# Splitting the first load of a half-rotary kernel into a one-row DMA and a fifteen-row DMA

## The chip, the cores and the metric

The kernel runs on one core of a Trainium2 chip. Its time is the device time of one execution in microseconds (us). Before the change three runs took 161.86, 161.61 and 161.78 us, a median of 161.78 us.

## What is computed

The input x has the shape (16, 512, 16, 64) in float32: batch, sequence, heads, dimension. cos and sin have the shape (512, 32), of which only the first 16 columns count. Of the 64 numbers of a head the first 32 are rotated in two halves of 16, and the last 32 are copied.

```python
x1, x2 = x[..., :32], x[..., 32:]
first  = x1[..., :16] * cos[..., :16] - x1[..., 16:] * sin[..., :16]
second = x1[..., :16] * sin[..., :16] + x1[..., 16:] * cos[..., :16]
return np.concatenate([first, second, x2], axis=-1)
```

So 33.55 MB are read and 33.55 MB are written, with about three operations for each rotated number.

## The kernel before

**Tiling.** x is seen as 16 x 512 = 8192 rows of 1024 floats (4 KB each). A tile t (0 to 3) is 128 partitions times K = 16 consecutive rows, so a partition of a tile is one contiguous run of 64 KB in memory, and a tile is 8.39 MB. Three tiles fit in the SBUF buffer `ring` (slot t mod 3); the fourth tile goes into slot 0 when tile 0 has been written out. `rows(t, lo, hi)` at L51 names rows lo to hi of a tile in all partitions, and `load` (L54) and `store` (L57) make one DMA of them.

**The DMA queues.** All loads and the stores of tiles 0, 1 and 3 are issued by SyncE (SP), in the order of the program; the page counts their packets under queue q1. The small loads of cos and sin (L63, L64) and the store of tile 2 are issued by GpSimd (POOL), under queue q0. Both queues are served by the same 16 DMA engines. An SP instruction that waits for a semaphore holds everything behind it on SP.

**The order of SP's work.** It issues load(0), load(1) and the second half of load(2) at once (L65 to L67). Then it waits for the rotated tile 0 and issues store(0) (L107), and behind it the first half of load(2) (L108). load(3) (L109) waits until store(0) has landed, since both use slot 0. store(1) (L112) is held by a dependency written out by hand (L118) until a part of tile 2 is rotated, so that it stands behind load(3) at the DMA engines. store(3) (L126) is the last.

**The tables.** The 64 KB of cos and of sin arrive in 32 partitions of `stage`. VectorE (DVE) waits for both (L73), shuffles and copies them (L73, L80, L83) into `table`, in which every partition has the 16 rows of cos and sin that belong to its 16 rows of x. This takes from 15.83 to 21.19 us of the profiled execution.

**The rotation.** `rotate(t, lo, hi)` (L90) is four DVE instructions on rows lo to hi: two products (L96, L97), a difference (L98) and a sum (L101). A half tile (8 rows) takes 4.43 + 4.42 + 2.29 + 2.28 us. The first product, L96, waits for the load of its rows; all later instructions follow on DVE in the program's order.

Of the kernel before, what the change touches and what calls it, by code (L numbers as in the profile page):

```python
# [1 line left out]

# [4 lines left out]


@with_exitstack
def kernel(  # L10
    ctx: ExitStack,
    tc: tile.TileContext,
    x: bass.AP,
    cos: bass.AP,
    sin: bass.AP,
    out: bass.AP,
):
    nc = tc.nc
    fp32 = mybir.dt.float32
    P = 128  # L20
    B, S, H, D = x.shape
    Q = D // 4
    HF = D // 2

    K = 16
    T = B * S // (P * K)
    PB = S // K
    REP = P // PB  # L30
    R = H * D
    NS = 3
    KC = K // 2
    KM = 5

    xf = x.rearrange("b s h d -> (b s h d)").rearrange("(t p f) -> t p f", t=T, p=P)
    of = out.rearrange("b s h d -> (b s h d)").rearrange("(t p f) -> t p f", t=T, p=P)
    cosf = cos.rearrange("(p k) j -> p (k j)", k=K)
    sinf = sin.rearrange("(p k) j -> p (k j)", k=K)

    const_pool = ctx.enter_context(tc.tile_pool(name="const", bufs=1))
    b_pool = ctx.enter_context(tc.tile_pool(name="bp", bufs=1, space=bass.MemoryType.PSUM))


    ring = const_pool.tile([P, NS, K, H, D], fp32)
    stage = const_pool.tile([P, 2, K, HF], fp32)
    spun = const_pool.tile([P, 2 * K, Q], fp32)
    packed = const_pool.tile([PB, 2 * K, Q], fp32)
    table = const_pool.tile([P, 2, K, 2, Q], fp32)

    def rows(t, lo, hi):  # L51
        return ring[:, t % NS, lo:hi].rearrange("p k h d -> p (k h d)")

    def load(t, lo=0, hi=K):  # L54
        return nc.sync.dma_start(out=rows(t, lo, hi), in_=xf[t, :, lo * R : hi * R])

    def store(t, lo=0, hi=K, queue=nc.sync):  # L57
        return queue.dma_start(out=of[t, :, lo * R : hi * R], in_=rows(t, lo, hi))  # L58


    nc.vector.memset(stage[:, :, :, 0:Q], 0.0)  # L61
    spread = stage.rearrange("(j b) t k i -> j b t (k i)", b=REP)
    nc.gpsimd.dma_start(out=spread[:, 0, 0], in_=cosf)  # L63
    nc.gpsimd.dma_start(out=spread[:, 0, 1], in_=sinf)  # L64
    load(0)  # L65
    load(1)
    load(2, KC, K)  # L67

    PQ = PB // REP
    nc.vector.stream_shuffle(  # L73
        out=spun[:],
        in_=stage.rearrange("p t k j -> p (t k) j")[:, :, 0:Q],
        mask=[j % PQ * REP for j in range(PB)],
    )
    for q in reversed(range(REP)):
        n = PQ * (q + 1)
        nc.vector.tensor_copy(out=packed[0:n], in_=spun[q * PB : q * PB + n])  # L80

    for r in range(REP):
        nc.vector.tensor_copy(  # L83
            out=table[r * PB : (r + 1) * PB].rearrange("p t k c j -> p (t k) c j"),
            in_=packed.unsqueeze(2).to_broadcast((PB, 2 * K, 2, Q)),
        )
    C = table[:, 0].rearrange("p k c j -> p k (c j)")
    Sn = table[:, 1].rearrange("p k c j -> p k (c j)")

    def rotate(t, lo, hi):  # L90
        x1 = ring[:, t % NS, lo:hi, :, 0:HF]
        c = C[:, lo:hi].unsqueeze(2).to_broadcast((P, hi - lo, H, HF))
        s = Sn[:, lo:hi].unsqueeze(2).to_broadcast((P, hi - lo, H, HF))
        b_full = b_pool.tile([P, KC, H, HF], fp32, name="b_t")
        b_t = b_full[:, 0 : hi - lo]
        nc.vector.tensor_mul(out=b_t, in0=x1, in1=s)  # L96
        nc.vector.tensor_mul(out=x1, in0=x1, in1=c)  # L97
        nc.vector.tensor_sub(  # L98
            out=x1[:, :, :, 0:Q], in0=x1[:, :, :, 0:Q], in1=b_t[:, :, :, Q:HF]
        )  # L100
        return nc.vector.tensor_add(  # L101
            out=x1[:, :, :, Q:HF], in0=x1[:, :, :, Q:HF], in1=b_t[:, :, :, 0:Q]
        )

    rotate(0, 0, KC)
    rotate(0, KC, K)
    store(0)  # L107
    load(2, 0, KC)  # L108
    load(3)  # L109
    rotate(1, 0, KC)  # L110
    rotate(1, KC, K)
    behind_loads = store(1)  # L112
    rotate(2, KC, K)
    near = rotate(2, 0, KM)
    rotate(2, KM, KC)
    store(2, queue=nc.gpsimd)

    tc.add_manual_dep(  # L118
        behind_loads.ins,
        near.ins.name,  # L120
        mybir.DependencyInfo(mybir.DependencyClass.Sync, mybir.DependencyReason.DATA),
        reason="the store follows the loads at the DMA engines",
    )
    rotate(3, 0, KC)
    rotate(3, KC, K)
    store(3)  # L126


# [1 line left out]
_INS = ['x', 'cos', 'sin']  # L130
_OUTS = [((16, 512, 16, 64), 'float32')]


# [23 lines left out]
```

## Time and profile before

| what | value |
|---|---|
| median of three runs | 161.78 us (161.61 to 161.86) |
| span of the profiled execution | 159.5 us |
| DVE busy | 112.9 us, 71% of the span |
| HBM read and written | 33.69 MB and 33.55 MB, 422 GB/s over the span |
| DMA packets | 1360, of which 176 under 512 bytes |
| first x load issued / first rotation starts | 0.74 us / 23.03 us |
| last rotation ends / span ends | 131.2 us / 159.5 us |

The span is the time from the first to the last recorded instruction of one profiled execution; the record gives no device time for that execution of its own, so the 2.28 us between its span and the median of the runs stand for what lies around it. Sums below are made against the span.

A DMA line of the profile gives packets, megabytes and the time that the packets took, as a share of 16 engines times the length of the stretch asked for. A packet is one piece that one DMA engine moves; the 64 KB of a partition are one packet here, and each DMA ends with one tiny packet on each engine that raises its semaphore. In a stretch a packet is counted with its whole duration if it starts there, so a share can exceed 100%.

### The profile page before, as it was taken

How to read it: one execution, taken by the hardware profiler on the slowest of the kernel's cores; microseconds unless marked ns; L12 is line 12 of the kernel's file. 1: busy time of each engine (PE TensorE's matmuls, PEld its weight loads, DVE VectorE, ACT ScalarE, POOL GpSimd, SP SyncE). 2: the span in 40 equal slices, each digit the busy share in tenths (PEclk: the TensorE clock that was granted, in tenths of full speed). 3: DMA queues.
4: the chain of work that ended last, by engine and by line, in shares of the span. 5: the costliest groups of instructions: out<-in, count | busy, mean ns of one | idle time of the engine just before them, and what ended most of it. 6: DMA issues, size and time to landing. Idle time of an engine off the chain costs nothing.

```text
span 159.5 us, 115 instructions
## 1 busy us (share of the span) xinstructions
DVE 112.9 (71%) x47; POOL 1.9 (1%) x7
## 2 busy tenths in 40 slices
DVE  1000959999999999999999999999999990000000
POOL 3000000000000000000000000010000000000000
DMA  7969979799699699699996996996996997999966
GB/s 263 542 263 542 444 345 526 345 444 526 271 493 551 279 510 526 263 394 411 510 526 263 526 526 263 526 526 263 526 526 263 526 460 329 526 394 394 526 263 263
DMA packets 1360, 67.24 MB, mean 422 GB/s; under 512 B 176, under 2 KB 176, under 8 KB 208
## 3 DMA queue, kind: packets, MB, share of 16 engines
q1 hardware_dynamic: 1152, 58.72, 85.7%
q0 software_dynamic: 208, 8.52, 12.4%
HBM read 33.69 MB, written 33.55 MB: 422 GB/s over the span
## 4 chain that ended last, share of the span: by engine, by line
DVE 61%; DMA 14%; issue 5%; DVEq 1%
DVE b_t L96 22%; DVE ring L97 22%; DMA ring<-in_x_dram 14%; DVE ring L101 10%; DVE ring L98 7%; DVEq L152 1%; DVEq L96 0%
## 5 line engine op out<-in xcount | busy, mean ns | idle before, releaser
L96 DVE TENSOR_TENSOR b_t<-ring,table 128x4096 f32<-128x4096 f32 (+2 forms) x9 | 35.6, 3959 | 2.1 <-DMA ring<-in_x_dram 1.8
L97 DVE TENSOR_TENSOR ring<-ring,table 128x4096 f32<-128x4096 f32 (+2 forms) x9 | 35.5, 3950 | 0.3
L98 DVE TENSOR_TENSOR ring<-ring,b_t 128x2048 f32<-128x2048 f32 (+2 forms) x9 | 18.4, 2049 | 0.3
L101 DVE TENSOR_TENSOR ring<-ring,b_t 128x2048 f32<-128x2048 f32 (+2 forms) x9 | 18.4, 2043 | 0.0
L73 DVE LOAD_MASK_SELECT spun<-stage x1 | 0.0, 14 | 14.4 <-DMA stage<-in_sin_dram 14.4
L83 DVE COPY table<-packed 32x1024 f32<-32x1024 f32 x4 | 2.7, 684 | 0.1
L58 POOL DMA_DIRECT2D out_dram<-ring x1 | 0.6, 562 | 101.7 <-DVE ring L101 101.7
L80 DVE COPY packed<-spun 32x512 f32<-32x512 f32 (+3 forms) x4 | 1.7, 416 | 0.1
L61 DVE MEMSET stage<- 128x512 f32 x1 | 0.5, 485 | 0.9 <-PEq L141 0.9
L73 DVE STREAM_SHUFFLE spun<-stage 128x512 f32<-128x512 f32 x1 | 0.7, 721 | 0.0
L63 POOL DMA_DIRECT2D stage<-in_cos_dram x1 | 0.6, 644 | 1.3 <-DVE stage L61 1.3
L64 POOL DMA_DIRECT2D stage<-in_sin_dram x1 | 0.5, 535 | 0.0
L141 POOL MEMSET const-bfloat16-1.0<- 128x1 bf16 x1 | 0.1, 102 | 0.0
L141 POOL MEMSET const-float32-0.0<- 128x1 f32 x1 | 0.1, 99 | 0.2 <-issue 0.2
L141 POOL MEMSET const-float32-1.0<- 128x1 f32 x1 | 0.1, 99 | 0.0
L141 POOL MEMSET const-uint8-127<- 128x1 uint8 x1 | 0.1, 99 | 0.0
## 6 DMA issues: line engine op xcount, KB each, us to landing
ring<-in_x_dram SPq DMA_DIRECT2D x2, 4096.0 KB, 40.7
stage<-in_cos_dram POOLq DMA_DIRECT2D x1, 64.0 KB, 9.0
stage<-in_sin_dram POOLq DMA_DIRECT2D x1, 64.0 KB, 13.3
ring<-in_x_dram SPq DMA_DIRECT2D x3, 29.0
out_dram<-ring SPq DMA_DIRECT2D x3, 27.4
out_dram<-ring POOLq DMA_DIRECT2D x1, 39.5
```

Of the source, the lines that this page charges most:

```text
L58: return queue.dma_start(out=of[t, :, lo * R : hi * R], in_=rows(t, lo, hi))
L61: nc.vector.memset(stage[:, :, :, 0:Q], 0.0)
L63: nc.gpsimd.dma_start(out=spread[:, 0, 0], in_=cosf)
L64: nc.gpsimd.dma_start(out=spread[:, 0, 1], in_=sinf)
L73: nc.vector.stream_shuffle(out=spun[:], in_=stage.rearrange("p t k j -> p (t k) j")[:, :, 0:Q], mask=[j % PQ * REP for j in range(PB)],)
L80: nc.vector.tensor_copy(out=packed[0:n], in_=spun[q * PB : q * PB + n])
L83: nc.vector.tensor_copy(out=table[r * PB : (r + 1) * PB].rearrange("p t k c j -> p (t k) c j"), in_=packed.unsqueeze(2).to_broadcast((PB, ...
L96: nc.vector.tensor_mul(out=b_t, in0=x1, in1=s)
L97: nc.vector.tensor_mul(out=x1, in0=x1, in1=c)
L98: nc.vector.tensor_sub(out=x1[:, :, :, 0:Q], in0=x1[:, :, :, 0:Q], in1=b_t[:, :, :, Q:HF])
L101: return nc.vector.tensor_add(out=x1[:, :, :, Q:HF], in0=x1[:, :, :, Q:HF], in1=b_t[:, :, :, 0:Q])
L152: with _tile.TileContext(nc) as tc:
```

## The change

The first load becomes two DMAs on the same queue, in the same place: first row 0 of each partition (128 runs of 4 KB), then rows 1 to 15 (128 runs of 60 KB). Everything else stays as it was. The first rotation needs rows 0 to 7, so L96 (L97 in the changed file) now waits for both semaphores, and so does store(0).

```diff
     nc.gpsimd.dma_start(out=spread[:, 0, 0], in_=cosf)
     nc.gpsimd.dma_start(out=spread[:, 0, 1], in_=sinf)
-    load(0)
+    load(0, 0, 1)
+    load(0, 1, K)
     load(1)
     load(2, KC, K)
```

In the built program SP has one DMA instruction more, ahead of the others; the instructions on DVE, GpSimd and the other engines are the same and in the same order.

## The prediction

> **What bounds the kernel now.** I read the page's DMA queues first, then the chain that ended last, because the two seem to disagree.
>
> ```profile
> span 159.5 us, 115 instructions
> q1 hardware_dynamic: 1152, 58.72, 85.7%
> q0 software_dynamic: 208, 8.52, 12.4%
> DVE 61%; DMA 14%; issue 5%; DVEq 1%
> ```
>
> The chain names DVE for 61% of the span. But the shares of the two queues add to 98.1%: each of the 16 DMA engines is busy for 156.5 of 159.5 us. The 3.0 us that are left lie at the two ends: no packet has started before 1.7 us, and the last ones end near 158.2 us by the trace's packet records, with a semaphore and the end of the program behind them. So there is practically no moment in between at which a DMA engine had nothing to do. The end is set by the sum of DMA work, as long as DVE delivers each store before the queue runs dry; DVE's chain is long, but it runs in step with the DMA work, not ahead of it.
>
> Next, the timeline of the start (start, duration, engine, line; in brackets the idle time before and what ended it) and, below the dots, of the first store:
>
> ```profile
> 0.74 1.33 SPq L55 DMA_DIRECT2D ring<-in_x_dram  x3
> ...
> 1.71 0.64 POOL L63 DMA_DIRECT2D stage<-in_cos_dram  x1 [1.26 <-DVE stage L61]
> 2.35 0.54 POOL L64 DMA_DIRECT2D stage<-in_sin_dram  x1
> 15.83 0.01 DVE L73 LOAD_MASK_SELECT spun<-stage  x1 [14.43 <-DMA stage<-in_sin_dram]
> ...
> 18.41 2.78 DVE L83 COPY table<-packed 32x1024 f32<-32x1024 f32 x4
> 23.03 4.43 DVE L96 TENSOR_TENSOR b_t<-ring,table 128x4096 f32<-128x4096 f32 x1 [1.85 <-DMA ring<-in_x_dram]
> ...
> 49.92 0.35 SPq L58 DMA_DIRECT2D out_dram<-ring  x1
> ```
>
> The reader is to see two things. The tables are ready at 18.41 + 2.78 = 21.19 us, and DVE then waits 1.85 us for x: load(0) lands last, not cos and sin. And from 23.03 us DVE works without a gap until it releases store(0) at 49.92 us.
>
> Last, the DMA queues in four short stretches: 1.7 to 4.7, 4.8 to 7.1, 7.1 to 9.6 and 50.9 to 51.7 us.
>
> ```profile
> q1 hardware_dynamic: 16, 1.05, 105.5%
> ```
> ```profile
> q1 hardware_dynamic: 15, 0.98, 98.6%
> ```
> ```profile
> q1 hardware_dynamic: 16, 1.05, 96.7%
> q0 software_dynamic: 16, 0.07, 6.4%
> ```
> ```profile
> DMA packets 32, 1.05 MB, mean 1311 GB/s; under 512 B 16, under 2 KB 16, under 8 KB 16
> ## 3 DMA queue, kind: packets, MB, share of 16 engines
> q1 hardware_dynamic: 32, 1.05, 303.7%
> ```
>
> A mean packet is the share times 16 times the stretch, over the packets. The first packet of each engine: 1.055 x 3.0 = 3.165 us. The second: 0.986 x 16 x 2.3 / 15 = 2.419 us. The third: 0.967 x 2.5 = 2.418 us. So the first pays 0.75 us to start the flow, and 64 KB then cost 2.42 us. The cos packets (16 packets, 0.07 MB, so 4 KB each) take 0.064 x 2.5 = 0.160 us. In the fourth stretch each engine ends the half load of tile 2 (16 semaphore packets) and starts store(0) (16 packets of 64 KB): 3.037 x 0.8 = 2.43 us for the pair. A seam between two queued DMAs thus costs about 0.01 us.
>
> **The change, part by part.**
>
> *Bytes and packets.* No byte is added. Each engine has 8 packets of 64 KB from load(0) now; it will have 8 of 4 KB, 8 of 60 KB and one semaphore packet more. By the two sizes above a byte costs (2.419 - 0.160) / 61,440 us, so 60 KB take 2.419 - 0.151 = 2.268 us. Eight rows: 8 x (0.160 + 2.268 - 2.419) = 0.07 us more, and 0.01 us for the seam. Sum: **0.08 us** per engine, all on the path, since the engines are never idle.
>
> *The start.* SP issues the first load at 0.74 us, and packets start from 1.75 to 2.5 us. I expect the small runs to start then too and to pay the same 0.75 us once; the train ends at about 1.75 + 0.75 + 8 x 0.160 = 3.8 us. The 60 KB load is issued one SP instruction later (three take 1.33 us, so 0.44 us), near 1.17 us, and its packets can start 1.0 to 1.8 us after that, by 3.0 us. So there is no hole at the seam, with 0.8 us to spare.
>
> No run of before shows a train of 4 KB packets, only single ones between large ones. From above: if each of the eight paid the starting 0.75 us by itself, 8 x 0.75 = 6.0 us. From below: if the small first packet did away with the 0.75 us, -0.75 us. I take 0.08 us, because the 0.160 us row is a packet of this very size; both ends are kept for the range.
>
> The Trainium skill, "DMA: Bandwidth & Descriptors", section "Bandwidth", speaks against the change: it asks for at least 1 MiB in a DMA, and its section "Anatomy of one DMA" fits 2.0 us plus bytes over 436 GB/s. Row 0 is 0.52 MB; by that rule it would cost 3.2 us instead of 1.2, and the run 2.0 us more. The seam of the fourth stretch above contradicts it for DMAs that wait in a queue, so I do not use it.
>
> *SP's issues.* load(1) and the half of load(2) are issued 0.44 us later, at about 1.6 and 2.1 us. They are needed at 23 and 43 us; nothing. Behind them SP waits for tile 0 until about 50 us anyway.
>
> *cos and sin.* The engines take the two queues in turn, packet by packet. In the second stretch (4.8 to 7.1 us) there is no q0 packet yet, in the third every engine serves cos first; so cos reached the engines between about 5 and 7.1 us. From there it takes three x packets more until sin's semaphore. With the change the 60 KB packets start at about 3.8 to 4.1, 6.1 to 6.4 and 8.3 to 8.7 us. If cos makes the 6.1 us turn, sin lands at 6.4 + 2 x 0.16 + 3 x 2.27 + 0.4 = 13.9 us; if it makes the next, 2.27 us later, at 16.2 us. It is 15.8 now. Tables ready 5.36 us later: 19.3 or 21.6 us. Load(0) lands at 22.94 + 0.08 = 23.0 us, after both. A table that is early by 2 us brings nothing: the wait for x covers it. The cover in the bad case is 23.0 - 21.6 = 1.4 us.
>
> *The added wait.* L97 of the changed file and store(0) wait for two loads instead of one. The first has landed near 4.5 us, so this is at most one more semaphore look, and the chain's DVEq pieces show 0.02 us for one. Behind L97 stands all of DVE's work. DVE starts about 0.1 us later, store(0) is issued about 0.1 us later, and the queue ahead of it drains 0.08 us later too. Packets start from 1.0 us after an issue, so store(0), issued at 49.92, is ready from 50.9 us, and the fourth stretch shows no hole at that seam. The margin may be as thin as 0.1 us, but load and drain shift together; I count 0 to 0.05 us.
>
> **Sum.** 159.5 + 0.08 to 0.13 us of span; with the 2.28 us around it, 161.78 + 0.1 = **161.9 us**. A measurement of this kernel can tell about 0.2% (0.32 us) from no change, so this is "no difference".
>
> **The rivals.**
>
> *The train of small runs stalls (slower).* Place: 1.75 to 4 us. The eight 4 KB packets do not follow each other at 0.160 us, or the 60 KB load behind them pays the starting 0.75 us again. For it: the only 4 KB packets in the profile travel alone, between 64 KB ones that keep the engine fed. Against it: nothing at those packets or at the seam shows a latency. It decides once a small packet costs over 0.19 us (8 x 0.03 + 0.08 = 0.32). With one more start of the flow: 161.78 + 0.08 + 0.75 = 162.6 us. All later work shifts by as much, since no engine has idle time to give back. Chance 0.22.
>
> *The tables become last (slower).* If cos misses two turns, sin lands at 18.5 us, the tables are ready at 23.8, 0.8 us behind x; store(0) then comes 0.8 us later than the drain allows, less a margin of 0.1 to 0.7 us: 162.0 to 162.6 us. Against it: cos was at the engines by 7.1 us in the record, so it makes the turn of 8.3. Chance 0.04.
>
> *The start becomes shorter (faster).* If the 0.75 us belong to the first 64 KB packet and not to the first access, small packets shorten it: down to 161.86 - 0.75 = 161.1 us. Against it: one engine starts at 2.5 us and needs no extra, which looks like one common delay until data flows, whatever the packet. Chance 0.14.
>
> *The split does not act as one.* The eight small runs of an engine could be moved as one piece. Then the added 0.07 us go too: 161.8 us. It is within the forecast's case.
>
> Whoever reads the chain alone (DVE 61%) would expect earlier tables to pull DVE forward; x lands last, so that gives 0.
>
> **Chances.** No difference 0.60 (the forecast and the merged runs), slower by over 0.2% 0.26, faster by over 0.2% 0.14. The forecast's own range is 161.6 to 162.1 us. For 8 in 10 I reach up to the second start of the flow, 162.6 us, and down to the middle of the faster case, 161.4 us; the far ends of the bounds (6.0 us more, 0.75 us less) stay outside.
>
> **What would show it.** In the profile after: 128 packets of 4 KB more on q1 and 16 more under 512 bytes; q1 and q0 together near 98%; the first rotation at 23.0 to 23.2 us, ended by x; DVE's wait for sin ending at 13.9 or 16.2 us. A first rotation over 0.3 us later, with x as releaser, shows the stalled train; with a table as releaser, the second rival; one at 22.7 us or before, the third. I am wrong if the 16 engines show idle time anywhere between 4 and 158 us that before does not have.

## The result and the profile after

The changed kernel took 163.01 us (median of four runs, 162.92 to 163.31) beside 161.69 us of the kernel before on the same chip. The ratio is 1.0089 with a 95% interval of 1.0072 to 1.0106: 1.3 us slower by the medians, 1.4 us by the ratio. The forecast was 161.9 us, and the range ended at 162.6 us.

The page of the changed kernel, the lines that answer to those shown of before:

```profile
span 161.1 us, 116 instructions
q1 hardware_dynamic: 1296, 58.72, 85.3%
q0 software_dynamic: 208, 8.52, 12.3%
DVE 61%; DMA 14%; issue 5%; DVEq 1%; SPq 0%
```

There are 144 more packets on q1, as counted beforehand (128 of 4 KB and 16 that raise a semaphore). The two shares add to 97.6% of 161.1 us, which is 157.2 us per engine: 0.7 us more than the 156.5 us of before, not 0.08 us. And the span has grown by 1.6 us, over twice that.

The timeline of the start and the first store (start, duration, engine, line; in brackets the idle time before):

```profile
0.74 1.84 SPq L55 DMA_DIRECT2D ring<-in_x_dram  x4
...
16.02 0.01 DVE L74 LOAD_MASK_SELECT spun<-stage  x1 [14.62 <-DMA stage<-in_sin_dram]
...
18.60 2.77 DVE L84 COPY table<-packed 32x1024 f32<-32x1024 f32 x4
24.34 4.43 DVE L97 TENSOR_TENSOR b_t<-ring,table 128x4096 f32<-128x4096 f32 x1 [2.96 <-DMA ring<-in_x_dram]
...
51.22 0.35 SPq L58 DMA_DIRECT2D out_dram<-ring  x1
```

The wait for sin ends at 16.02 us, near the later of the two values forecast. x is still last. But the first rotation starts at 24.34 us, 1.31 us later than before, and store(0) is issued 1.30 us later. In this execution a delay nearly as large as the whole loss stands at the first rotation already.

The issues of the two parts of load(0), with the time from issue to the landing on the last engine:

```profile
ring<-in_x_dram SPq DMA_DIRECT2D x1, 7680.0 KB, 23.1
ring<-in_x_dram SPq DMA_DIRECT2D x1, 512.0 KB, 4.6
```

Row 0 was issued at 0.74 us and landed on its last engine at 5.3 us, where the forecast had it near 4.5; rows 1 to 15, issued at 1.16, landed at 24.2 us. The trace records when each of the 16 engines raises a DMA's semaphore. For load(0) of the kernel before these times run from 22.36 to 22.94 us, with a mean of 22.67. In the changed kernel they run from 22.59 to 24.21, mean 23.14. The mean engine is 0.47 us late; the last one is 1.27 us late.

The train of 4 KB packets comes first. Here are the stretch from 2.35 to 3.55 us, in which only 4 KB packets of x start, and the shorter one from 3.25 to 3.6 us:

```profile
q1 hardware_dynamic: 73, 0.30, 74.4%
```
```profile
q1 hardware_dynamic: 33, 0.14, 93.7%
```

The first gives 0.744 x 16 x 1.2 us / 73 = 0.196 us for a packet, the second 0.937 x 16 x 0.35 / 33 = 0.159 us, the price of the forecast. The first is higher because it still holds the start of the flow: by the packet records the early packets of an engine took up to 1.31 us. All eight of an engine, the start included, took 1.98 us on average (2.06 and 1.87 us in two further profiles of this kernel, below), against 0.75 + 8 x 0.160 = 2.03 us in the forecast. So the train is not what makes the mean engine late. But it leaves the engines apart: they start their first 60 KB packet between 3.61 and 4.97 us, 4.02 on average, where the forecast had 3.8 to 4.1. (In the kernel before the first packets end between 4.73 and 5.36 us.)

What follows the train costs more than forecast. The stretch from 10.9 to 11.2 us, in which sin is served:

```profile
q1 hardware_dynamic: 4, 0.25, 190.6%
q0 software_dynamic: 7, 0.03, 40.5%
```

The sin packets, 4 KB each, take 0.405 x 16 x 0.3 / 7 = 0.28 us here, and the x packets beside them 1.906 x 16 x 0.3 / 4 = 2.29 us instead of 2.27. Before, cos and sin packets took 0.159 us, every one. By the packet records the longer packets between 3.6 and 17 us add 0.33 us to an engine (0.24 and 0.47 us in the two further profiles; nothing in the kernel before). With the 0.08 us of the forecast that is most of the 0.47 us; the rest is that the first packets started 0.06 us later on average.

### The profile page after: what moved, and what is told of

It is laid out like the page before. It is cut to its first block, busy times and chain, and to the rows that moved or that the text cites. A ratio compares the mean times of both kernels' runs of the same rounds, so it can differ in the third digit from the quotient of the medians.

```text
span 161.1 us, 116 instructions
## 1 busy us (share of the span) xinstructions
DVE 112.9 (70%) x47; POOL 1.9 (1%) x7
## 4 chain that ended last, share of the span: by engine, by line
DVE 61%; DMA 14%; issue 5%; DVEq 1%; SPq 0%
DVE b_t L97 22%; DVE ring L98 22%; DMA ring<-in_x_dram 14%; DVE ring L102 10%; DVE ring L99 7%; DVEq L153 1%; SPq L55 0%; DVEq L97 0%
## 5 line engine op out<-in xcount | busy, mean ns | idle before, releaser
L97 DVE TENSOR_TENSOR b_t<-ring,table 128x4096 f32<-128x4096 f32 (+2 forms) x9 | 35.6, 3959 | 3.2 <-DMA ring<-in_x_dram 3.0
## 6 DMA issues: line engine op xcount, KB each, us to landing
ring<-in_x_dram SPq DMA_DIRECT2D x1, 7680.0 KB, 23.1
```

## The experiments

Theory A at the start: the row-0 train is uneven over the engines, DVE waits for the last of them, and the others run dry before store(0). Rival B: there is simply more DMA work. Rival C came up with the first results: the cos and sin packets, which take turns with the 60 KB packets, throw the engines out of step. After the first four runs theory A became A2 and then A3, as the expectations say. The table gives for each kernel the ratio to the kernel before, and how much later than before the last and the mean engine raised the semaphore of the whole load(0) (22.94 and 22.67 us before) and of the last DMA, store(3) (158.61 and 158.44 us), in the one profiled execution.

| kernel | ratio (95% interval) | load(0): last, mean | end: last, mean |
|---|---|---|---|
| changed kernel | 1.0089 (1.0072 to 1.0106) | +1.27, +0.47 | +1.48, +1.34 |
| again | 1.0086 (1.0071 to 1.0101) | +0.75, +0.39 | +1.40, +0.87 |
| again2 | one run, 162.31 us | +0.65, +0.45 | +0.66, +0.65 |
| late_dve | 1.0074 (1.0059 to 1.0089) | -0.11, -0.04 | +1.07, +1.06 |
| row0_last | 1.0100 (1.0071 to 1.0128) | +0.58, +0.24 | +1.55, +0.71 |
| split1 | 1.0022 (1.0012 to 1.0032) | +0.28, 0.00 | +0.56, +0.33 |
| first2 (8 KB + 56 KB) | 1.0013 (1.0001 to 1.0025) | -0.14, -0.28 | -0.09, -0.12 |
| first4 (16 KB + 48 KB) | 1.0038 (1.0006 to 1.0070) | -0.17, -0.09 | +0.93, 0.00 |
| first8 (32 KB + 32 KB) | 1.0075 (1.0059 to 1.0091) | -0.21, -0.08 | +0.85, +0.71 |
| first12 (48 KB + 16 KB) | 1.0070 (1.0054 to 1.0086) | +0.22, +0.09 | +1.06, +0.63 |
| row15_last (60 KB + 4 KB) | 1.0059 (1.0038 to 1.0079) | +0.36, +0.26 | +0.11, -0.11 |
| after_deep | 1.0113 (1.0093 to 1.0134) | +1.20, +0.51 | +2.14, +1.45 |
| before_deep | 1.0013 (1.0003 to 1.0023) | -0.01, 0.00 | +0.26, +0.01 |
| dummy64 | 1.0215 (1.0173 to 1.0256) | +1.27, +1.13 | +3.35, +2.21 |
| dummy4 | 1.0215 (1.0176 to 1.0253) | +1.29, +1.04 | +3.80, +2.02 |
| notab_split | 0.9991 (0.9981 to 1.0000) | +0.14, +0.01 | +0.18, +0.17 |
| notab_whole | 0.9971 (0.9959 to 0.9984) | -0.14, -0.39 | -0.11, -0.14 |
| tab_in_order | 1.0201 (1.0183 to 1.0219) | +1.06, +0.97 | +3.15, +1.80 |

**The changed kernel again.**

> The changed kernel once more, as a control. Theory A (the row-0 train runs unevenly at the start, the slowest DMA engine sets when DVE may begin, and the other engines run dry before store(0)): again about 163.0 us, load(0) landing on its last engine over 0.8 us later than on its mean engine, and idle DMA time of 0.3 us or more per engine just before store(0). Theory B (all engines simply have more DMA work): about 163.0 us, but landing spread and idle time as in the kernel before.

162.91 us. The last engine was 0.63 us behind the mean one at load(0), not over 0.8, and the engines idled only 0.08 us on average just before store(0) (0.40 us in the first profile). Neither sign of theory A is there. Yet the time was the same: in this execution the rest of the loss came at the load behind store(0), whose last engine landed 1.38 us later than before.

> One more look at the changed kernel, for how far its landing spread differs between executions: two profiles showed the last engine of load(0) 1.27 and 0.75 us later than in the kernel before. Theory A3: again 0.6 us or more, 162.8 to 163.3 us.

162.31 us in its one run, below the range given; the last engine 0.65 us late at load(0), and 0.66 us late at the end. Three profiles of one kernel thus show +1.27, +0.75 and +0.65 us. The issue lines of the two repeats, for rows 1 to 15 (issued at 1.16 us):

```profile
ring<-in_x_dram SPq DMA_DIRECT2D x1, 7680.0 KB, 22.5
```
```profile
ring<-in_x_dram SPq DMA_DIRECT2D x1, 7680.0 KB, 22.4
```

**A late DVE alone.** The kernel before, with

```diff
+    early = ring[:, 0, 0:4, :, 0:HF]
+    nc.vector.tensor_copy(out=early, in_=early)
     rotate(0, 0, KC)
```

> The kernel before with one DVE copy of a part of tile 0 onto itself ahead of the first rotation; by the row of the table copies (0.684 us for 1024 elements a partition) it delays DVE by about 1.3 us, as the late landing did, and leaves the DMA work as it was. Theory A: store(0) comes 1.3 us late, the queue runs dry by 0.9 to 1.2 us, 162.6 to 163.0 us. Theory B (the sum of DMA work decides): 161.7 us.

162.77 us, as theory A expected. The timeline shows the copy and the first rotation behind it, and then the issue of store(0):

```profile
22.86 1.23 DVE L106 COPY ring<-ring 128x2048 f32<-128x2048 f32 x1 [1.78 <-DMA ring<-in_x_dram]
24.12 4.43 DVE L96 TENSOR_TENSOR b_t<-ring,table 128x4096 f32<-128x4096 f32 x1
...
51.00 0.35 SPq L58 DMA_DIRECT2D out_dram<-ring  x1
```

In the stretch from 50.9 to 51.7 us, where the kernel before ended the half load of tile 2 and started store(0) on all 16 engines, this kernel has:

```profile
DMA packets 16, 0.00 MB, mean 0 GB/s; under 512 B 16, under 2 KB 16, under 8 KB 16
## 3 DMA queue, kind: packets, MB, share of 16 engines
q1 hardware_dynamic: 16, 0.00, 1.1%
```

Only the 16 semaphore packets: the queue has run dry. The load(0) of this kernel landed as before, so DVE's 1.09 us (24.12 against 23.03) by themselves cost 1.2 us (0.74% of 161.62). Part of it is idle time: 0.63 us per engine before store(0), by the packet records. Another part comes at the end of store(0), where its last 64 KB packets, one per engine, stand. In the kernel before (67.5 to 70.5 us), in this kernel and in the changed one (both 67.5 to 71 us):

```profile
q1 hardware_dynamic: 16, 1.05, 92.1%
```
```profile
q1 hardware_dynamic: 16, 1.05, 90.7%
```
```profile
q1 hardware_dynamic: 16, 1.05, 90.0%
```

That is 0.921 x 3.0 = 2.76 us a packet before, 0.907 x 3.5 = 3.17 us here and 0.900 x 3.5 = 3.15 us in the changed kernel, where a 64 KB packet takes 2.418 us elsewhere.

**Row 0 behind rows 1 to 15.** The two new lines of the change swapped.

> The same two DMAs in the other order: rows 1 to 15 first, then row 0, so the small runs come at about 22 us into a flow that is already running. Theory A: the train then takes 8 x 0.16 us on every engine, and the time is that of the kernel before plus 0.1 us, 161.7 to 162.0 us. Theory B (more work, wherever it stands): 163.0 us.

163.22 us: a miss. With the small runs at 21 us instead of at the start the mean engine is only 0.24 us late at load(0), but the last one 0.58 us, and the last engine is 1.48 us late at the load behind store(0). Theory A as first put, in which only the start of the flow matters, fell here.

**More work ahead of store(0).** The changed kernel, and below it the kernel before, with

```diff
-    load(2, KC, K)
+    load(2, KC - 1, K)
...
-    load(2, 0, KC)
+    load(2, 0, KC - 1)
```

> The changed kernel with one row of tile 2 moved from the load behind store(0) to the load ahead of it (9 rows ahead, 7 behind), which gives every engine 1.2 us more work before store(0) is needed. Theory A: the idle time of 0.40 us per engine before store(0) goes, and 162.2 to 162.7 us is left, since the slow start itself stays. Theory B: no idle time is at stake, 163.0 us.

> The kernel before with the same shift of one row of tile 2 ahead of store(0) as in after_deep (9 rows ahead in 36 KB runs, 7 behind in 28 KB runs). If the shift is harmless by itself: 161.3 to 161.8 us, and after_deep was a fair test of the idle time before store(0). If the 28 KB runs or the deeper queue cost something: 162.1 us or more, and after_deep says nothing on the idle time.

The idle time before store(0) went (0.02 us per engine), but the time rose to 163.55 us, a miss for theory A, while the shift alone costs 0.13%. The semaphore times show that some of the delay was won back and then lost again. At load(0) the last engine was 1.21 us behind that of before_deep, at the end of store(0) only 0.61 us (73.75 against 73.14; the changed kernel is 1.25 us behind the kernel before there). But in the load behind store(0) the 28 KB packets took 0.62 us per engine longer than their usual 1.062 us each (0.01 us in before_deep), and it ended 1.87 us behind. So this run doesn't tell what the idle time alone is worth.

**The same packets in load(1).** The kernel before, with load(1) split into row 0 and rows 1 to 15.

> The kernel before with load(1), not load(0), split into row 0 and rows 1 to 15: the same 128 + 128 packets in a running flow, with no cos and sin packets beside them and DVE's start untouched. Theory A2 (short and odd-sized packets cost the 16 engines unevenly wherever they stand; an engine that falls behind never catches up, and the last one ends the kernel): the landing spread of the engines grows from 0.6 to about 0.9 us at load(1) and stays, 162.0 to 162.6 us. Rival C (the 60 KB packets are disturbed by the cos and sin packets between them, and DVE starts late): nothing of that is here, 161.7 us.

161.83 us, between the two ranges given: +0.22%. In the stretch from 22.2 to 23.2 us, in which the train runs:

```profile
DMA packets 104, 0.39 MB, mean 385 GB/s; under 512 B 10, under 2 KB 10, under 8 KB 104
...
q1 hardware_dynamic: 104, 0.39, 94.3%
```

Without the 10 semaphore packets that is 0.943 x 16 x 1.0 / 94 = 0.160 us a packet: in a running flow, without cos and sin, the train costs what the forecast took. The 60 KB packets behind it took 2.296 us on average instead of 2.267, which adds 8 x 0.029 = 0.23 us to each engine.

**Where the split stands.** `load(0, 0, n)` and `load(0, n, K)` with n = 2, 4, 8, 12 and 15.

> The split after row 1: 8 KB runs, then 56 KB runs, between the changed kernel (4 KB, 163.0 us) and the one with 16 KB (161.7 us). If the length of the short runs at the start counts: 162.0 to 162.8 us, last landing of load(0) 0.2 to 0.9 us later than before. If 4 KB alone is bad: as with 16 KB, 161.5 to 161.9 us.

161.60 us: runs of 8 KB cost 0.13%, next to nothing. So at the front of load(0) it is the 4 KB runs that cost, not short runs in general. The first rotation starts earlier than before:

```profile
17.08 2.77 DVE L84 COPY table<-packed 32x1024 f32<-32x1024 f32 x4
22.93 4.43 DVE L97 TENSOR_TENSOR b_t<-ring,table 128x4096 f32<-128x4096 f32 x1 [3.07 <-DMA ring<-in_x_dram]
```

The tables are ready at 19.85 us, 1.3 us earlier than before, and it brings nothing, since x lands last.

> The split after row 3 instead of row 0: 16 KB runs, then 48 KB runs. Theory A3 (a train of very short runs into engines that are not yet flowing leaves them out of step, the last engine's landing of load(0) sets DVE's start, and a late DVE costs nearly its whole delay): with 0.6 us packets the engines come through more evenly, last landing of load(0) at most 0.6 us later than before, 161.8 to 162.6 us. Rival (any second DMA on load(0) costs about the same): 162.9 us and a last landing of 23.6 us or later.

161.68 us, but the ten runs reach from 161.25 to 163.61 us. load(0) landed 0.17 us earlier than before; in the profiled execution two engines then lost 0.6 to 0.7 us at the load behind store(0) and 0.3 us more in load(3).

> load(0) split into rows 0 to 7 and rows 8 to 15, 32 KB packets in both. The first rotation then needs the first half alone and can start when the tables are ready, at about 21.2 us. Theory A2: 32 KB packets run evenly (1.213 us each in the kernel before), so the spread stays at 0.6 us and the time is 161.3 to 161.8 us. If any split of load(0) puts the engines out of step: spread of 0.9 us or more and over 162.3 us.

162.69 us: a miss, and not for the reason offered: load(0) landed with a spread of 0.43 us, narrower than before. DVE started at 17.33 us and store(0) was issued at 44.22 us, 5.7 us earlier. Then the last 32 KB loads ahead of store(0), from 48.6 to 49.1 us, ran slowly:

```profile
q1 hardware_dynamic: 16, 0.52, 393.1%
```

3.931 x 0.5 = 1.97 us for a packet that takes 1.213 us elsewhere.

> The split after row 11: 48 KB runs (which ran evenly in the kernel with 16 and 48 KB), then 16 KB runs in a running flow. The first rotation needs the first part alone, so DVE can start when the tables are ready, near 20 us. If an early DVE and even packets are what counts: faster than before, 160.9 to 161.4 us. If store(0) queued well ahead brings a loss of its own, as in the kernel split after row 7: 161.8 us or more.

162.85 us: the same again. The packets ran evenly, DVE started at 18.36 us, store(0) was issued at 45.25 us, and the 32 KB loads ahead of it lost 1.0 us per engine. An early DVE does not gain.

> The split at the other end: rows 0 to 14 in 60 KB runs, then row 15 in 4 KB runs. The small runs stand in a running flow, and the first rotation needs the 60 KB part alone, so DVE can start about 1.2 us earlier than before, at about 21.8 us. Theory A3: the spread at the end of the train is 0.9 us as in row0_last, but DVE does not wait for it; 161.2 to 161.9 us. Rival (the split costs DMA time, whatever DVE does): 162.5 to 163.2 us as in row0_last.

162.28 us, a miss by 0.4 us; the ten runs reach from 161.89 to 163.25 us, and the profiled one is the fastest, so its landings do not stand for the others.

**A train ahead of a whole load(0).** The kernel before with one DMA more at the front, from row 0 of every partition, or from one contiguous piece:

```diff
+    nc.sync.dma_start(out=rows(2, 0, 1), in_=xf[0, :, 0:R])
     load(0)
```

> The kernel before with one DMA more at the start: row 0 of tile 0 is read in 128 runs of 4 KB at a pitch of 64 KB into a row of the buffer that is overwritten later; load(0) then goes whole. If the train ran evenly it would add 8 x 0.16 = 1.3 us to every engine: 163.0 us. Theory D (runs that lie 64 KB apart get in each other's way): mean small packet well over 0.16 us, landing spread of load(0) 0.9 us or more, 163.4 to 164.2 us. Theory that a train at the start is uneven by itself: the same here as in the next kernel.

> As dummy64, but the 128 runs of 4 KB are one contiguous piece of memory. Theory D: the train runs evenly, the landing spread of load(0) stays at 0.6 us, 162.9 to 163.1 us. Theory that a train at the start is uneven by itself: spread of 0.9 us or more and 163.4 to 164.2 us, as in dummy64.

165.12 and 165.00 us: no difference between 64 KB apart and contiguous, so theory D falls. In both the last landing of load(0) is 1.27 to 1.29 us late, just the added work (8 x 0.159 + 0.009 = 1.28), with 0.60 and 0.79 us between the first and the last engine (0.58 before): a 4 KB train ahead of 64 KB packets hardly puts the engines out of step at load(0). Over 2 us more were lost on the last engine from store(0) on (about 1.0 us on the mean one), most of it by the end of the load behind it; neither expectation had that.

**Without cos and sin.** The two loads left out, the memset with 1.0 instead of 0.0.

> The changed kernel without the loads of cos and sin; the tables are filled with ones on the chip, so this kernel leaves out the reading of cos and sin and its output is not the rotation asked for. Without the 0.34 us of their packets an undisturbed load(0) would land on its last engine at 22.94 + 0.08 - 0.34 = 22.7 us. Rival C (the cos and sin packets between the 60 KB packets put the engines out of step): 22.6 to 22.9 us and a spread of 0.6 us. Theory A3: 23.2 us or later, spread 0.9 us or more.

161.47 us in its one run; the last landing at 22.95 us, 0.25 us over the undisturbed value, spread 0.52 us. That lies between the two ranges, nearer to C's.

> The changed kernel without the reading of cos and sin (tables of ones, so the output is not the rotation asked for), timed against the kernel before and, in the same call, against the next kernel. One profile of it showed the last landing of load(0) at 22.95 us. Theory A3: 0.5 us or more slower than the next kernel. Rival C: at most 0.3 us slower than the next kernel.

> The kernel before without the reading of cos and sin (tables of ones, as in the kernel above). It has 0.34 us of DMA work less, so the last landing of load(0) should be near 22.6 us and the time 161.0 to 161.3 us by either theory; it is the base of the kernel above.

161.52 against 161.21 us: without the cos and sin packets the split costs 0.31 us instead of 1.3 to 1.4, just beyond C's 0.3 and short of A3's 0.5. The issue line of rows 1 to 15 (again at 1.16 us):

```profile
ring<-in_x_dram SPq DMA_DIRECT2D x1, 7680.0 KB, 21.9
```

It lands at 23.1 us; with cos and sin it was 23.6 to 24.2, of which their own packets are 0.34 us. The 60 KB packets are slow here too. The stretch from 10.4 to 11.4 us of notab_split, with one on each engine:

```profile
q1 hardware_dynamic: 16, 0.98, 240.2%
```

That is 2.402 x 1.0 = 2.40 us instead of 2.267; between 3.6 and 17 us it comes to 0.43 us per engine. So the mean engine lands load(0) 0.40 us later than in notab_whole, as much as the 0.39 to 0.47 us with cos and sin. What is missing here is the rest: the last engine is 0.28 us later than in notab_whole and DVE starts 0.31 us later (23.21 against 22.90), no more than the mean engine, and no engine idles before store(0).

> The changed kernel with the loads of cos and sin issued by SP between row 0 and rows 1 to 15, so that they stand in the same queue at the same place on every engine and nothing is served in turn any more. Rival C (the turn-taking between the cos and sin packets and the 60 KB packets puts the engines out of step): last landing of load(0) 23.0 to 23.2 us, spread 0.6 us, time 161.5 to 161.9 us. Theory A3 alone (the train of 4 KB runs at the start and the 60 KB packets do it): last landing 23.5 us or later, 162.3 us or more.

164.97 us, and inconclusive: SP issued rows 1 to 15 only at 2.62 us, behind the wait for the memset, so the train drained and the flow started twice (0.51 us idle per engine up to 6 us, against 0.31 us). It changed more than the turn-taking.

## Why the prediction was wrong

**The bound** was named rightly: the DMA engines are busy from 1.7 to 158 us, and x, not the tables, is last before the first rotation. Earlier tables brought nothing (first2).

**"Sum: 0.08 us per engine"** is the first term that failed: the mean engine landed load(0) 0.39 to 0.47 us later. The price of the train was right: with the start of the flow it took 1.87 to 2.06 us per engine, and the forecast had 2.03. What was mis-sized is what comes behind it. The 60 KB packets, put at 2.268 us, took 2.28 to 2.30 us on average, and the cos and sin packets between them 0.21 to 0.25 us instead of 0.160. The 2.268 us had been worked out between two sizes that the kernel before moves without disturbance. The 60 KB packets were also slow without cos and sin (notab_split) and in load(1) (split1).

**"Load and drain shift together; I count 0 to 0.05 us"** is the step that cost most. It treats 16 engines as one. Each engine moves its own sixteenth of every DMA, and up to store(0) it had no idle time, so an engine that fell behind stayed behind: in the changed kernel the last engine was late by 1.27, 1.26 and 1.26 us at load(0), load(1) and the half load of tile 2. DVE waits for the last engine; the early ones drain on nearly the old schedule. So DVE was late by 1.31 us against a queue whose mean engine was late by 0.47, and the engines idled 0.40 us each before store(0). That is the idle time that the prediction had named as its sign of being wrong. What a late DVE costs was measured by itself: 1.2 us for 1.09 us. But idle time is only a part of this cost. The late store(0) also came with slower packets where the queue goes from store(0) to the load behind it, a term that the prediction did not have. Counted by the packet records, in us per engine more than in the kernel before (after_deep: than in before_deep), the three parts add up to how late the mean engine ends:

| profile | late at load(0) | idle before store(0) | slower packets, 67.5 to 77 us | sum | late at the end |
|---|---|---|---|---|---|
| changed kernel | 0.47 | 0.40 | 0.41 | 1.28 | 1.34 |
| again | 0.39 | 0.08 | 0.39 | 0.86 | 0.87 |
| again2 | 0.45 | 0.02 | 0.17 | 0.64 | 0.65 |
| late_dve | -0.04 | 0.63 | 0.41 | 1.00 | 1.06 |
| after_deep | 0.51 | 0.02 | 0.96 | 1.49 | 1.44 |

So where the forecast counted 0 to 0.05 us, the three profiles of the changed kernel show 0.81, 0.47 and 0.19 us in the second and third part, and at the end the last engine is later than the mean one by up to 0.5 us more than in the table. late_dve, in which only DVE is late, has the third part too. But kernels that issue store(0) at 49.8 to 49.9 us differ there from 0.10 to 0.69 us, so that a late store(0) makes these packets slow is likely, not shown.

**The part on cos and sin** (an early table brings nothing, a late one has 1.4 us of cover) was right for the tables and wrong for the x packets. Nothing that sets the end waited for cos and sin, but their packets are part of the trouble: without them the split costs 0.31 us, with them 1.3 to 1.4. They do not make the mean engine later (0.40 us without them), but the last one. In the changed kernel cos was served by 14 engines behind their first 60 KB packet, from 5.95 us on, and by two a packet later, at 8.2 us (its semaphore was raised between 8.75 and 11.03 us, before between 10.09 and 10.70). It takes both, however: with 8 KB runs and the same cos and sin packets the cost is 0.13%.

**The rivals.** The stalled train (chance 0.22) had the sign and the place at the start, but not the mechanism: once the start of the flow is taken off, a small packet took 0.159 us, under the 0.19 us from which that rival was to decide, and the 60 KB load did not pay the start a second time. What it had foreseen as its sign, a first rotation over 0.3 us later with x as releaser, came by the last engine. Late tables did not occur. The shorter start did occur, with 8 KB runs: the mean engine landed 0.28 us earlier, and the end did not follow.

The rule of the Trainium skill, "DMA: Bandwidth & Descriptors", section "Bandwidth", that speaks against DMAs under 1 MiB had the sign. Its size, by the fixed 2.0 us that the section "Anatomy of one DMA" gives for a DMA issued by GpSimd, is not what the runs show for one queued by SP: the same 0.52 MB DMA costs 0.31 to 0.35 us in notab_split and split1.

**What stays open.** Why a 4 KB train into engines that are only starting leaves them 0.7 to 1.4 us apart (first starts of a 60 KB packet, three profiles) where an 8 KB train leaves 0.33, why the 60 KB packets behind it are slow, and how cos and sin make the last engine later, was not settled: tab_in_order changed too much. Also open is a second loss around 68 to 75 us, where the queue goes from store(0) to the load behind it. There the packets of an engine took 0.41 us longer than usual in the kernel before, 0.58 to 0.82 us in the changed one, 0.82 us in late_dve, and 1.1 to 1.3 us in dummy4 and dummy64. It tends to be larger the later store(0) is issued (0.04 us in row15_last, with store(0) at 48.94 us); before_deep, at 0.10 us with store(0) at 49.91 us, and notab_whole, at 0.69 us with store(0) at 49.79 us, do not fit.

## What to carry to other kernels

Where every DMA engine is busy all the time, do not add up DMA work for a mean engine: read the semaphore times of all 16, because the compute engine waits for the last one, and here that one kept its delay of 1.27 us over three loads. Before a long mean is put down to the price of a packet, take off the start of the flow: the stretch at the start gave 0.196 us, and the packets behind the start took 0.159. Look instead at what stands next to the new packets; here that was the 60 KB packets. And measure the margin by delaying the compute engine alone: here a delay of 1.1 us cost 1.2 us, of which the idle time before store(0) is only about half.

## What the runs showed that was not expected

- A start of DVE that is too early went with as much loss as a late one. With store(0) issued 4.7 to 5.7 us earlier than in the kernel before (first12, first8), the last two 32 KB packets of each engine in the load ahead of it took 1.7 to 1.8 us on average instead of 1.213, and the kernel was 0.70 to 0.75% slower. None of the kernels tried was faster than the one before with the same outputs.
- A 4 KB run is one packet in the train from SP (128 runs, 128 packets), while cos and sin from GpSimd, 64 runs of 2 KB, travelled as 32 packets of 4 KB. In tab_in_order, issued by SP, they were 64 packets of 2 KB.
- 1.28 us of additional DMA work at the very front (dummy4, dummy64) cost 3.5 us (2.15% of 161.48).
